# Keys' norm ahead of the scores, one normalisation for eight heads, and a first threshold search counted by ScalarE alone

## The chip, the cores and the metric

One core of a Trainium2 chip runs the whole kernel in one launch. The metric is the device time in microseconds. TensorE (PE) multiplies, VectorE (DVE) and ScalarE (ACT) work on elements, GpSimd (POOL) does the small updates of the threshold search, and SyncE (SP) issues the transfers.

## The reference

The input is 1024 tokens of 1024 features. Two layers of a first block come first, then one second block (a gated recurrence, a chunked linear attention and an MLP), which the change doesn't touch. A layer of the first block, cut to what matters:

```python
def first_block(x, c, ...):
    for l in range(DEPTH):                       # 2
        h = rmsnorm(x, g_pre[l]) * (1.0 + scale) + shift
        p = h @ w_in[l]
        u_val, u_gate, g_conv, c_q, c_kv, k_idx, w_idx, g_attn = jnp.split(p, offsets, axis=-1)
        y_conv = conformer_conv(u_val, u_gate, ...) * jax.nn.silu(g_conv)
        y_attn = dsa_attention(c_q, c_kv, k_idx, w_idx, ...) * jax.nn.silu(g_attn)
        y = jnp.concatenate([y_conv, y_attn], axis=-1) @ w_out[l]
        x = x + gate * rmsnorm(y, g_post[l])

def dsa_attention(...):                          # blocks of 128 queries, 8 heads
    cq = rmsnorm(c_q, q_norm_g)
    kv = rmsnorm(c_kv, kv_norm_g)                # the keys' norm
    score = jnp.einsum("bth,bths->bts", w_b, jax.nn.relu(s_raw))
    _, sel = lax.top_k(score, 256)               # of the keys up to the query
    logits = q . kv[sel] * KV_LORA ** -0.5 + bias
    probs = jax.nn.softmax(logits)
    o = (probs . kv[sel]) @ w_uv                 # 64 outputs a head
```

## The kernel before

SBUF is cut into 50 pages of 1024 words a partition. A page is handed out and freed by the program in the order in which its code is emitted; a page that is freed and handed out again makes its new writer wait for its old readers. fp32 products are three matmuls of a high and a low part (`split`, L262 to L265; `mm3`, L267 to L271). A scheduler puts the emitted instructions of each engine into one fixed order ahead of the run. What it starts from is the order in which generators are woven (`weave`), with rates, gates and priorities in the tables `RATES`, `GATES` and `PRIOR`.

A layer makes the inputs of a convolution, then the latents of queries, keys and index keys (`g_latents`, six units), then index scores for the blocks 2 to 7 of 128 queries (`g_scores`, L844 to L859; the blocks 0 and 1 have at most 256 keys and need no choice). A threshold for each query is searched bit by bit on the two 16-bit halves of the scores, 31 bits in all (`g_topk`). There are two searches a layer, one for the blocks 2, 3 and 4 and one for 5, 6 and 7. In each bit the keys of a block at or above a candidate are counted. The table `GROUPS` says by whom: in the first search block 2 (384 keys) by VectorE (L921, updates in L926, L929 and L931), and blocks 3 and 4 (512 and 640 keys) by ScalarE as a sum of signs (L913), with GpSimd making the next candidate out of the count:

```python
nc.gpsimd.tensor_scalar(hn, half, nxt, None, op0=OP.add)                        # L916
nc.gpsimd.tensor_scalar(tm, cnt, lim, -step, op0=OP.is_gt, op1=OP.mult)         # L917
nc.gpsimd.tensor_tensor(half, tm, hn, op=OP.add)                                # L919
```

In the second search VectorE counts blocks 5 and 6 (768 and 896 keys) and ScalarE block 7. A search ends with the threshold as a float, the choice of ties by a running count, and the mask (L956 to L979). Its pages are freed late, that is, handed out again from the attention on.

After the scores the keys are normed (`norm_keys`: ScalarE's square, a matmul of ones in L302, ScalarE's logarithm L294 and exponential L297, a product), split, and multiplied into the values (L1010). Queries of all heads follow, with both searches running beside. Then comes the attention, a block of 128 queries at a time, in pairs of heads: logits (L1116 to L1124), minimum with the mask (L1130; for the blocks 0 and 1 L1134 and L1137), exponential with its sum (L1138), the reciprocal of the two sums (L1141), its broadcast over 64 rows by two matmuls (L1145), the product with the gate (L1147), transposes (L1154) and their copies (L1158, L1160), the values (L1164), and the final product (L1168). The attention of blocks 0 to 4 has the second search woven in.

## Time and profile before

| | |
|---|---|
| three runs | 3029.22, 3030.16, 3030.83 us |
| median | 3030.16 us |
| span of the profiled execution, its only time on record | 3029.3 us |
| PE, PEld, DVE, ACT, POOL busy | 2906.8, 2362.8, 2229.9, 1679.8, 247.2 us |
| HBM read, written | 201.21, 60.29 MB |

Busy time is that of instructions on an engine; a busy TensorE may still run at its lower clock, which the slices and the windows of the trace give beside it (PEclk, 1.00 is 2.4 GHz and 0.50 is 1.2 GHz). A wait is idle time of an engine just before an instruction, with the instruction that ended it.

### The profile page before, as it was taken

How to read it: one execution, taken by the hardware profiler on the slowest of the kernel's cores; microseconds unless marked ns; L12 is line 12 of the kernel's file. 1: busy time of each engine (PE TensorE's matmuls, PEld its weight loads, DVE VectorE, ACT ScalarE, POOL GpSimd, SP SyncE). 2: the span in 40 equal slices, each digit the busy share in tenths (PEclk: the TensorE clock that was granted, in tenths of full speed). 3: DMA queues.
4: the chain of work that ended last, by engine and by line, in shares of the span. 5: the costliest groups of instructions: out<-in, count | busy, mean ns of one | idle time of the engine just before them, and what ended most of it. 6: DMA issues, size and time to landing. Idle time of an engine off the chain costs nothing.

```text
span 3029.3 us, 40735 instructions
## 1 busy us (share of the span) xinstructions
PE 2906.8 (96%) x15235; PEld 2362.8 (78%) x15235; DVE 2229.9 (74%) x4118; ACT 1679.8 (55%) x3032; POOL 247.2 (8%) x630
## 2 busy tenths in 40 slices
PE   9998787999999888999999999999999999999999
PEld 6877565778877665777888888888888888888887
DVE  5998899776988899756555667656666587776875
ACT  6248766737147866646444466555555654454454
POOL 0005511000005511000000000000000000000000
PEclk9999989999999989999999999999999999999999
DMA  8222102154101200133122211101013344456443
GB/s 276 63 40 63 42 18 77 48 193 149 39 18 42 63 19 18 36 112 118 49 62 62 79 35 36 56 29 56 29 37 122 103 143 153 151 201 238 153 146 111
DMA packets 218637, 264.14 MB, mean 87 GB/s; under 512 B 11504, under 2 KB 153543, under 8 KB 218439
## 3 DMA queue, kind: packets, MB, share of 16 engines
q1 hardware_dynamic: 218438, 261.54, 26.7%
q8 instruction: 119, 1.95, 0.3%
q14 instruction: 80, 0.65, 0.1%
HBM read 201.21 MB, written 60.29 MB: 86 GB/s over the span
## 4 chain that ended last, share of the span: by engine, by line
PE 58%; DVE 5%; POOL 2%; ACT 2%; DMA 1%; issue 1%; POOLq 0%; ACTq 0%
PE ps L269 15%; PE ps L271 15%; PE ps L270 15%; PE ps L331 5%; PE ps L1499 2%; DVE pg L921 2%; POOL consts L917 1%; PE ps L1164 1%; PE ps L1154 1%; POOL consts L919 1%; POOL consts L916 1%; DMA pg<-in_w_in_dram 1%; PE ps L1488 0%; DVE pg L1130 0%; PE ps L498 0%
## 5 line engine op out<-in xcount | busy, mean ns | idle before, releaser
L269 PE MATMUL ps<-pg,pg 128*128 128x512 f32 (+2 forms) x3080 | 1178.7, 384 | 15.1 <-DVE pg L265 4.2
L270 PE MATMUL ps<-pg,pg 128*128 128x512 f32 (+2 forms) x3080 | 1176.3, 383 | 0.0
L271 PE MATMUL ps<-pg,pg 128*128 128x512 f32 (+2 forms) x3080 | 1176.0, 382 | 0.0
L264 ACT ACTIVATE pg<-pg 128x512 fp32r<-128x512 f32 (+2 forms) x884 | 481.7, 591 | 527.7 <-PE ps L271 157.2
L269 PEld LDWEIGHTS ps<-pg,pg 128*128 128x128 f32 x3080 | 580.5, 189 | 132.9 <-DVE pg L265 10.1
L271 PEld LDWEIGHTS ps<-pg,pg 128*128 128x128 f32 x3080 | 580.6, 189 | 109.8 <-issue 3.7
L270 PEld LDWEIGHTS ps<-pg,pg 128*128 128x128 f32 x3080 | 580.8, 189 | 107.9 <-issue 3.5
L265 DVE TENSOR_TENSOR pg<-pg,pg 128x512 fp32r<-128x512 f32 (+2 forms) x884 | 528.2, 636 | 136.4 <-ACT pg L264 121.3
L278 POOL TENSOR_TENSOR consts<-consts 128x1 f32<-128x1 f32 x56 | 31.3, 559 | 2069.0 <-DVE consts L277 2069.0
L913 ACT ACTIVATE pg<-pg,consts 128x512 bf16<-128x512 uint16 (+5 forms) x186 | 166.8, 897 | 40.8 <-POOL consts L919 36.1
L703 DVE SCALAR_TENSOR_TENSOR pg<-pg,consts,pg 128x512 f32<-128x512 f32 (+15 forms) x256 | 176.9, 742 | 0.4
L331 PE MATMUL ps<-pg,pg 128*128 128x512 f32 x768 | 175.9, 389 | 0.0
L921 DVE TENSOR_SCALAR_CACHE_REDUCE pg<-pg,consts 128x384 bf16<-128x384 uint16 (+5 forms) x186 | 170.9, 919 | 2.3
L331 PEld LDWEIGHTS ps<-pg,pg 128*128 128x128 f32 x768 | 143.8, 188 | 29.6
L1138 ACT ACTIVATE pg<-pg,consts 128x256 f32<-128x256 f32 (+7 forms) x128 | 98.9, 774 | 70.2 <-DVE consts L1130 51.7
L1154 PE MATMUL ps<-consts,pg 128*128 128x128 f32 x576 | 107.7, 291 | 1.9 <-ACT pg L1160 1.1
L852 PE MATMUL ps<-pg,pg 128*128 128x512 f32 (+3 forms) x320 | 86.3, 370 | 14.7 <-DVE pg L844 9.4
L1164 PE MATMUL ps<-pg,pg 128*64 128x128 f32 x1152 | 92.5, 292 | 5.8 <-DVE pg L1147 1.7
L1116 PE MATMUL ps<-pg,pg 128*128 128x384 f32 (+5 forms) x192 | 79.4, 415 | 16.2 <-DVE consts L1130 7.9
L1160 ACT ACTIVATE pg<-ps 128x512 f32<-128x512 f32 (+1 forms) x112 | 57.8, 532 | 66.8 <-PE ps L1154 62.4
L917 POOL TENSOR_SCALAR consts<-consts 128x1 f32<-128x1 f32 x186 | 78.0, 419 | 179.1 <-ACT pg L913 173.5
L1164 PEld LDWEIGHTS ps<-pg,pg 128*64 128x64 f32 x1152 | 64.1, 141 | 35.1 <-issue 13.4
(350 smaller groups left out, 3810.7 us busy)
## 6 DMA issues: line engine op xcount, KB each, us to landing
pg<-in_w_in_dram SPq DMA_DIRECT2D x104, 512.0 KB
pg<-hidden SPq DMA_DIRECT2D x56, 512.0 KB
hidden<-pg SPq DMA_DIRECT2D x48, 512.0 KB
pg<-in_w_ada_dram SPq DMA_DIRECT2D x32, 512.0 KB
pg<-in_w_up_dram SPq DMA_DIRECT2D x32, 512.0 KB
pg<-in_w_down_dram SPq DMA_DIRECT2D x32, 512.0 KB
pg<-in_w_out_dram SPq DMA_DIRECT2D x24, 512.0 KB
x<-pg SPq DMA_DIRECT2D x24, 512.0 KB
```

Source lines behind the costliest of these rows:

```text
L264: self.nc.scalar.activation(hi, src, AF.Copy)
L265: self.nc.vector.tensor_sub(lo, src, hi.bitcast(F32))
L269: nc.tensor.matmul(ps, lhsT=wl, rhs=rh, start=first, stop=False)
L270: nc.tensor.matmul(ps, lhsT=wh, rhs=rl, start=False, stop=False)
L271: nc.tensor.matmul(ps, lhsT=wh, rhs=rh, start=False, stop=last)
L331: nc.tensor.matmul(ps, lhsT=w[z][k], rhs=act[y][k][:, a:b], start=k + n == 0, stop=3 * k + n == 3 * kt - 1)
L703: nc.vector.scalar_tensor_tensor(out, x[:, :512 - d], w, prev[:, d:], op0=OP.mult, op1=OP.add)
L913: nc.scalar.activation(junk_a(b), keys[b], AF.Sign, scale=-1.0, bias=col(tk["half"], b), accum_out=col(tk["cnt"], b))
L917: nc.gpsimd.tensor_scalar(col(tk["tm"], b), col(tk["cnt"], b), lim, -step, op0=OP.is_gt, op1=OP.mult)
L921: nc.vector.tensor_scalar(junk_d(b), keys[b], col(tk["cand"], b), None, op0=OP.is_ge, op1=OP.add, accum_out=col(tk["cnt"], b))
L1154: nc.tensor.transpose(pt[:, c:c + 128], Ps[hi][:, j * 128:j * 128 + 128], self.ident)
L1164: nc.tensor.matmul(uv[hi * 64:hi * 64 + 64], lhsT=V[j // 2][:, v:v + 64], rhs=th[:, jj * 256 + hi * 128:jj * 256 + hi * 128 + 128], start= ...
```

## The change

Three parts, and docstrings and comments taken out, which shifts line numbers.

- The keys' norm becomes a seventh unit of `g_latents`, ahead of the scores, with the page and the function table of that generator; `norm_keys` goes.
- The attention gathers the sums of all eight heads of a block in one [128, 8] tile. Reciprocal, broadcast, gate product and final product happen once a block, at the last pair of heads. The values of the four pairs share one PSUM bank.
- `GROUPS` hands block 2 of the first search to ScalarE, in both layers, so that VectorE counts none there. GpSimd's update takes two operations.

```diff
-GROUPS = ((([2], [3, 4]), ([5, 6], [7])), (([2], [3, 4]), ([5, 6], [7])))
+GROUPS = ((([], [2, 3, 4]), ([5, 6], [7])), (([], [2, 3, 4]), ([5, 6], [7])))
...
-            self.sums = [self.const(2) for _ in range(4)]
+            self.sums = [self.const(8) for _ in range(2)]
...
         def g_latents():
...
+            for s in halves:
+                sq = t[:, s]
+                nc.scalar.activation(sq, kv[:, s], AF.Square)
+                ps = self.bank("t", s4)
+                self.sum_rows(ps, [sq])
+                self.bcast_rstd(sq, ps, 128, tab)
+                nc.vector.scalar_tensor_tensor(kv[:, s], kv[:, s], self.vec[f"kv_norm_g{l}"][:, 0:1], sq, op0=OP.mult,
+                                               op1=OP.mult)
+            yield
             self.free(t, cq)
...
-                        nc.gpsimd.tensor_scalar(col(tk["hn"], b), col(tk["half"], b), nxt, None, op0=OP.add)
                         nc.gpsimd.tensor_scalar(col(tk["tm"], b), col(tk["cnt"], b), lim, -step, op0=OP.is_gt,
                                                 op1=OP.mult)
-                        nc.gpsimd.tensor_tensor(col(tk["half"], b), col(tk["tm"], b), col(tk["hn"], b), op=OP.add)
+                        nc.gpsimd.tensor_scalar(col(tk["half"], b), col(tk["half"], b), col(tk["tm"], b), nxt, op0=OP.add,
+                                                op1=OP.add)
...
-        weave((pr(g_latents(), 9), 6), bg=[(conv, RATES[l][1])])
+        weave((pr(g_latents(), 9), 7), bg=[(conv, RATES[l][1])])
...
-        norm_keys()
...
-                    nc.vector.reciprocal(sm, sm)
-                    pu = self.bank("pu", [6])
-                    uv, rb = pu[:, :128], pu[:, 128:256]
-                    for hi in range(2):
-                        nc.tensor.matmul(rb[hi * 64:hi * 64 + 64], lhsT=sm[:, hi:hi + 1].to_broadcast([128, 64]),
-                                         rhs=self.ident, start=True, stop=True)
-                    nc.vector.tensor_mul(gb[:, hp], gb[:, hp], rb)
+                    uv = uvs[:, hp * 128:hp * 128 + 128]
+                    if hp == 3:
+
+                        nc.vector.reciprocal(sm, sm)
+                        rb = self.bank("pt", [4, 5])
+                        for h in range(8):
+                            nc.tensor.matmul(rb[h % 2 * 64:h % 2 * 64 + 64, h // 2 * 128:h // 2 * 128 + 128],
+                                             lhsT=sm[:, h:h + 1].to_broadcast([128, 64]), rhs=self.ident, start=True,
+                                             stop=True)
+                        nc.vector.tensor_mul(gb, gb, rb)
...
                     self.free(Ps)
-                    nc.vector.tensor_mul(yb[:, hp], uv, gb[:, hp])
+                    if hp == 3:
+                        nc.vector.tensor_mul(yb, uvs, gb)
```

What moves is best seen in the order of the instructions. VectorE at the fifth and sixth heads of attention block 0 of layer 0, before; `pg25_220` and `pg28_221` are the pages of their exponentials, `pg18_209` takes the bits of a count, `pg7_212` and `pg6_211` hold keys of the second search, and `consts_58` stands for all small columns:

```order
L1134 TENSOR_TENSOR pg25_220_3075<-ps_62,consts_58 128x128
L1141 RECIPROCAL consts_58<-consts_58 128x2
L921 TENSOR_SCALAR pg18_209_2801,consts_58<-pg7_212_2804,consts_58 128x768
L1137 TENSOR_REDUCE consts_58<-pg25_220_3075 128x1
L921 TENSOR_SCALAR pg18_209_2801,consts_58<-pg6_211_2803,consts_58 128x896
L1147 TENSOR_TENSOR pg8_214_2987<-pg8_214_2987,ps_62 128x128
L1141 RECIPROCAL consts_58<-consts_58 128x2
L929 TENSOR_SCALAR consts_58<-consts_58 128x2
L931 SCALAR_TENSOR_TENSOR consts_58<-consts_58 128x2
L1134 TENSOR_TENSOR pg28_221_3092<-ps_62,consts_58 128x128
L1168 TENSOR_TENSOR pg38_215_2989<-ps_62,pg8_214_2987 128x128
L1137 TENSOR_REDUCE consts_58<-pg28_221_3092 128x1
```
Between the fifth head's logits and the sixth's there are two counts and the small steps of one bit. The same engine with the change, where L985 to L990 are the end of the first search (L974 to L979 before), `pg26_147` and `pg17_148` pages of that search, `pg16_132` a page of scores, and L1131 and L1134 the logits and the minimum:

```order
L978 TENSOR_SCALAR consts_58<-consts_58 128x1
L985 TENSOR_SCALAR pg26_147_1710<-pg16_132_1364,consts_58 128x640
L986 SCALAR_TENSOR_TENSOR pg17_148_1711<-consts_58,pg26_147_1710 128x640
L988 TENSOR_SCALAR pg16_132_1364<-pg16_132_1364,consts_58 128x640
L989 SCALAR_TENSOR_TENSOR pg26_147_1710<-pg17_148_1711,consts_58,pg26_147_1710 128x640
L990 SCALAR_TENSOR_TENSOR pg16_132_1364<-pg26_147_1710,pg16_132_1364 128x640
L1131 TENSOR_TENSOR pg17_221_3027<-ps_62,consts_58 128x128
L1131 TENSOR_TENSOR pg26_220_3006<-ps_62,consts_58 128x128
L1134 TENSOR_REDUCE consts_58<-pg17_221_3027 128x1
```
The sixth head's page is `pg26_220`, the place of the first search's `pg26_147`, and the seventh's is `pg17_221`, the place of `pg17_148`; both are written behind the last step of the first search.

ScalarE among the latents of layer 1, before; L294 and L297 are the logarithm and the exponential of a norm, L689 the gates, L264 splits, L843 copies of index queries:

```order
L294 ACT_TABLE_LOAD
L294 ACTIVATE pg14_485_6772<-ps_62,consts_58 128x512
L297 ACT_TABLE_LOAD
L297 ACTIVATE pg14_485_6772<-pg14_485_6772 128x512
L264 ACTIVATE pg4_481_6768<-pg32_473_6618 128x512
L264 ACTIVATE pg13_482_6769<-pg25_474_6619 128x512
L726 ACTIVATE pg14_495_7144<-pg27_487_6809 128x15
L689 ACT_TABLE_LOAD
L689 ACTIVATE pg6_493_6850<-ps_62 128x512
L843 ACTIVATE pg18_492_6837<-ps_62 128x384
```
And with the change, where L808 is the square of the keys' norm:

```order
L294 ACT_TABLE_LOAD
L294 ACTIVATE pg14_484_6604<-ps_62,consts_58 128x512
L808 ACTIVATE pg14_484_6604<-pg15_460_6303 128x512
L297 ACT_TABLE_LOAD
L297 ACTIVATE pg14_484_6604<-pg14_484_6604 128x512
L294 ACT_TABLE_LOAD
L294 ACTIVATE pg14_484_6604<-ps_62,consts_58 128x512
L297 ACT_TABLE_LOAD
L297 ACTIVATE pg14_484_6604<-pg14_484_6604 128x512
L264 ACTIVATE pg4_480_6600<-pg23_472_6450 128x512
L264 ACTIVATE pg24_481_6601<-pg25_473_6451 128x512
L808 ACTIVATE pg14_484_6604<-pg15_460_6303 128x512
```
A gate of the conv branch (L689) lies in the middle of norms in both, and with the change a load of a function table stands ahead of every logarithm and every exponential here.

## Rows read from the trace of the kernel before

**Rows 1.** The page: the span, the busy time by engine with its share of the span and the number of instructions, and, out of the slices, PE's busy tenths and its granted clock.

```profile
span 3029.3 us, 40735 instructions
...
PE 2906.8 (96%) x15235; PEld 2362.8 (78%) x15235; DVE 2229.9 (74%) x4118; ACT 1679.8 (55%) x3032; POOL 247.2 (8%) x630
...
PE   9998787999999888999999999999999999999999
...
PEclk9999989999999989999999999999999999999999
```
**Rows 2.** The timeline of ScalarE, start and duration in us: the last score's eviction, the first and the sixth exponential of attention block 0, in layer 0.

```profile
313.50 1.01 ACT L854 ACTIVATE pg<-ps 128x1024 f32<-128x1024 f32 x1
...
397.09 0.40 ACT L1138 ACTIVATE pg<-pg,consts 128x128 f32<-128x128 f32 x1 [1.31 <-DVE consts L1137]
...
406.91 0.40 ACT L1138 ACTIVATE pg<-pg,consts 128x128 f32<-128x128 f32 x1 [0.65 <-DVE consts L1137]
```
**Rows 3.** Busy time of each engine in the four stages of layer 0 that these starts cut, and of layer 1 cut at the same instructions: the length, then PE, weight loads, DVE, ACT, POOL with their instructions, PE's granted clock, the DMA share and GB/s.

```profile
232.50:314.50 82.00, 73.02 (x319) 58.76 (x318) 69.62 (x162) 66.50 (x132) 51.80 (x113) 0.98 0.20 58
...
314.50:397.10 82.60, 60.28 (x220) 42.10 (x219) 70.70 (x169) 66.30 (x131) 38.80 (x109) 0.89 0.14 42
...
397.10:406.90 9.80, 7.68 (x37) 6.15 (x35) 9.37 (x33) 4.14 (x14) 0.64 (x3) 0.50 0.01 2
...
406.90:506.80 99.90, 86.89 (x637) 64.63 (x637) 95.05 (x302) 66.65 (x151) 14.76 (x59) 0.90 0.18 53
...
925.00:1007.40 82.40, 74.74 (x336) 60.80 (x335) 76.94 (x181) 69.98 (x142) 59.62 (x128) 1.00 0.20 61
...
1007.40:1080.50 73.10, 59.99 (x223) 42.75 (x221) 61.92 (x146) 60.27 (x119) 31.53 (x92) 0.90 0.15 48
...
1080.50:1094.70 14.20, 11.53 (x57) 8.87 (x56) 13.59 (x45) 7.19 (x21) 1.92 (x9) 0.50 0.00 0
...
1094.70:1200.00 105.30, 89.69 (x636) 62.88 (x635) 98.31 (x316) 72.36 (x161) 14.58 (x56) 0.96 0.06 18
```
**Rows 4.** Waits in total, number and longest: from 200 to 560 us (layer 0) three of PE and one of ScalarE, then from 880 to 1220 us (layer 1) two of PE.

```profile
PE ps L302 <- ACT pg L294: 12.6, 1, 12.6
...
PE ps L1145 <- DVE consts L1141: 7.5, 8, 1.6
...
PE ps L852 <- DVE pg L844: 3.8, 5, 1.2
...
ACT pg L913 <- POOL consts L919: 17.7, 24, 1.5
...
PE ps L302 <- ACT pg L294: 8.3, 1, 8.3
...
PE ps L1145 <- DVE consts L1141: 8.9, 10, 2.2
```
**Rows 5.** The timeline of PE around the matmul of ones, layer 0.

```profile
346.24 2.07 PE L302 MATMUL ps<-pg,consts 128*128 128x512 f32 x2 [12.62 <-ACT pg L294]
...
349.39 0.63 PE L270 MATMUL ps<-pg,pg 128*128 128x512 f32 x1
...
349.82 0.63 PE L271 MATMUL ps<-pg,pg 128*128 128x512 f32 x1
...
354.87 0.39 PE L270 MATMUL ps<-pg,pg 128*128 128x512 f32 x1
```
**Rows 6.** The timeline of ScalarE: two counts, of 512 and of 640 keys, and a table load with what starts behind it.

```profile
252.59 0.71 ACT L913 ACTIVATE pg<-pg,consts 128x512 bf16<-128x512 int16 x1
...
254.00 0.82 ACT L913 ACTIVATE pg<-pg,consts 128x640 bf16<-128x640 int16 x1
...
193.34 1.28 ACT L689 ACT_TABLE_LOAD   x1
...
194.63 0.60 ACT L689 ACTIVATE pg<-ps 128x512 f32<-128x512 f32 x1
```
**Rows 7.** Groups of VectorE's instructions from 200 to 560 us, shapes apart: total busy, mean ns of one, idle time before.

```profile
L921 DVE TENSOR_SCALAR_CACHE_REDUCE pg<-pg,consts 128x384 bf16<-128x384 uint16 x16 | 9.7, 606 | 0.2
...
L921 DVE TENSOR_SCALAR_CACHE_REDUCE pg<-pg,consts 128x768 bf16<-128x768 int16 x15 | 15.1, 1008 | 0.3
...
L921 DVE TENSOR_SCALAR_CACHE_REDUCE pg<-pg,consts 128x896 bf16<-128x896 int16 x15 | 17.1, 1141 | 0.2
...
L1147 DVE TENSOR_TENSOR pg<-pg,ps 128x128 f32<-128x128 f32 x25 | 7.1, 284 | 2.1 <-PE ps L1145 1.7
...
L1168 DVE TENSOR_TENSOR pg<-ps,pg 128x128 f32<-128x128 f32 x24 | 6.9, 286 | 1.2 <-PE ps L1164 1.1
...
L1158 DVE COPY pg<-ps 128x512 f32<-128x512 f32 x10 | 6.8, 686 | 2.2 <-PE ps L1154 1.8 <-PE ps L1164 0.5
...
L1141 DVE RECIPROCAL consts<-consts 128x2 f32<-128x2 f32 x25 | 4.0, 159 | 0.0
```
**Rows 8.** The timeline of VectorE in layer 1: the first and the last step of the end of the first search.

```profile
1039.23 0.17 DVE L934 TENSOR_SCALAR consts<-consts 128x2 f32<-128x2 f32 x1 [2.02 <-POOL consts L919]
...
1051.84 0.82 DVE L979 SCALAR_TENSOR_TENSOR pg<-pg,pg 128x640 f32<-128x640 bf16 x1
```
**Rows 9.** Groups of GpSimd's instructions from 200 to 560 us.

```profile
L916 POOL TENSOR_SCALAR consts<-consts 128x1 f32<-128x1 f32 x93 | 34.9, 376 | 65.3 <-DVE consts L952 36.2 <-DVE consts L902 21.5
...
L919 POOL TENSOR_TENSOR consts<-consts 128x1 f32<-128x1 f32 x93 | 32.2, 347 | 7.8
```

More of the change, by code (lines that the diff above doesn't have):

```diff
@@ L981, in g_topk @@
             self.free(cnt_pg, kps, late=True)
-        def norm_keys():
-            kv = lat["kv"]
-            t = self.page()
-            tab = self.ln_table()
-            for s in halves:
-                sq = t[:, s]
-                nc.scalar.activation(sq, kv[:, s], AF.Square)
-                ps = self.bank("k", [3])
-                self.sum_rows(ps, [sq])
-                self.bcast_rstd(sq, ps, 128, tab)
-                nc.vector.scalar_tensor_tensor(kv[:, s], kv[:, s], self.vec[f"kv_norm_g{l}"][:, 0:1], sq, op0=OP.mult,
-                                               op1=OP.mult)
-            self.free(t)
         def split_keys():
```

16 lines of the change are left out of this document (9 added, 7 removed).

## The prediction

> **What bounds the kernel now.** I read the page first: busy time by engine, then the slices. PE is busy 2906.8 of 3029.3 us [rows 1], so the whole reads as a kernel bound by TensorE, and an edit that takes work from VectorE or ScalarE seems worth nothing. The slices say more: PE falls to 7 or 8 tenths in slices 4 to 7 and 14 to 16, and its granted clock to 8 tenths in slices 6 and 15 [rows 1]. The change touches only the sparse attention of the two layers, so I cut those two pieces into four stages by what starts on ScalarE [rows 2], the end of the last score's eviction, the first, and the sixth exponential of attention block 0, and took the busy time of each engine in each stage [rows 3]. What the reader is to see there, layer 0: the scores (82.00 us, PE 73.02); from the last score to the first exponential (82.60 us, with PE 60.28, VectorE 70.70 and ScalarE 66.30, so no engine full, and the clock at 0.89); the first five heads (9.80 us, VectorE 9.37, clock 0.50, which is the lower level, 1.2 GHz); then attention proper (99.90 us, VectorE 95.05, PE 86.89). Layer 1 is alike: 82.40, 73.10, 14.20, 105.30. Last I read which wait PE names in them [rows 4]: one wait of the ones-matmul of the keys' norm for ScalarE's logarithm, 12.6 and 8.3 us, and the reciprocal's broadcast for VectorE, 7.5 and 8.9 us. Behind the long wait PE runs at the lower clock: matmuls of a 512-wide product start 0.43 us apart and take 0.63 each, and only from 354.87 on 0.39 [rows 5], so of the 8.6 us from 346.24 some 3 are lost as well.
>
> **Part by part.** All sums stand against the profiled span of 3029.3 us; the median of the runs is 3030.16, so I add 0.9 at the end.
>
> Keys' norm. Its place between the scores and the values goes, and with it the wait: in layer 0 12.6 + 3 = 15.6 us of a stage that otherwise held 67 us; in layer 1 8.3 + about 2 by the stage's clock of 0.90. What is late next in this stage is ScalarE. I walked ScalarE's order of the changed kernel with the durations of the trace: a Sign count takes 0.71 us at 512 keys, 0.82 at 640 [rows 6], thus an estimated 0.61 at 384. From the last score to the first exponential this sums to 60.5 us in layer 0 (64.2 before), 59.3 in layer 1 (59.1 before): fewer bits of the old blocks, but one count more in each bit. VectorE falls from 66.6 to 39.5 us there. With ScalarE filled to 95% (VectorE reaches 95.05 of 99.90 where it sets the pace [rows 3]) the stage takes about 64 us in layer 0 and 63 in layer 1. That is -18 and -10; bounds -20 and -8 in layer 0 (the latter if the counts wait for GpSimd as now, 17.7 us in all [rows 4]), -13 and -2 in layer 1.
>
> In its new place the norm has Square, two ones-matmuls, logarithm, exponential, scale. The work is the same, but ScalarE's order shows other loads of function tables: one less in layer 0, three more in layer 1, where gates of the conv branch fall between logarithm and exponential. A load takes 1.28 us and the next activation starts 1.29 us after it [rows 6]. So -1.3 and +3.8 us of ScalarE time; since the index latents wait for ScalarE just there, and a wait of PE brings the lower clock behind it, I take +2 and +5; bounds 0 and +8 each.
> The Trainium skill (ScalarE: Activation LUTs, What ACT_TABLE_LOAD costs) gives 1283 ns for the load and about 1380 ns of drain on top, 2.66 us in all. The row agrees with the load and shows no drain behind it; by the rule the two net loads would be worth an estimated 5.3 us, by the row 2.6.
>
> One normalisation for eight heads. Per block of 128 queries four gate products of 0.284 us, four final products of 0.286 and four reciprocals of 0.159 [rows 7], 2.9 us of VectorE, become one each. A 512-wide product out of PSUM isn't in the trace; nearest is the 512-wide copy out of PSUM, 0.686, and four times the narrow one, 1.14, is the other bound. So 0.16 + 2 x 0.686 = 1.5 us, a gain of 1.4 us a block (0.5 at the other bound), 11 us for eight blocks. Matmul count stays at eight 128x128 broadcasts. On PE's path the waits for the reciprocal (7.5, 8.9) go for three pairs in four.
>
> Counts to ScalarE. 31 counts of 384 keys with their updates leave VectorE: the 0.61 of a count less the overlap of 0.08, the update's share, some 27 us a layer with the normalisation by VectorE's order summed with traced durations (2023 to 1969 us over both layers). 31 x 0.61 = 19 us a layer come to ScalarE. ScalarE has the room in total, but not in the last 60 us ahead of attention. So the first search ends later: before, its last count lies some 36 us of ScalarE work ahead of the first exponential; now it lies 14 and 7 us behind it. This meets memory. The page of the sixth head of attention block 0 is the one that holds the counts and the ties of the first search (page 26), and VectorE's new order has the whole end of that search, L985 to L990 for three blocks, ahead of the sixth head's logits. So five heads start as early as they can and the sixth waits. VectorE's work from first to sixth head is 9.3 us before and 30.4 (layer 1: 31.4) now: six or seven bits of the second search, a 768 and an 896 count of 1.01 and 1.14 us with updates each [rows 7], and the end of the first search, from 1039.23 to 1052.66 in layer 1 with 2 us of other work in it [rows 8]. At 95% and with a handover to ScalarE and back: 34 us and 35 us where there were 9.80 and 14.20, +24 and +21. Bounds +20 and +17 (VectorE full) to +28 and +26. PE has nothing else to do there.
> What VectorE does in that gap it need not do later: by the order, seven to eight bits of the second search are done early, 2.25 us each, 17 us, and 11 us come from the normalisation. But behind the sixth head PE is soon the bound: 86.89 busy of 99.90 at clock 0.90, so 78 us at full clock and 22 to be had; in layer 1 89.69 at 0.96 of 105.30, 86 and 19. Of it I take two thirds, -15 and -13, since the start still runs at the low clock after the gap; the least is the reciprocal's wait, -8 each, the most -22 and -19.
>
> GpSimd. Three operations become two, but with three blocks six remain for each bit. Their first (hn, mean 0.376 us [rows 9]) was already done beside the count, off the path; the last, 0.347, becomes a form with a pointer. I take 0; a path shorter or longer by 0.1 us over 31 bits gives 3 us a layer at most either way. Scores: VectorE freer, PE waits for its share of copies 3.8 us now [rows 4]; ScalarE gets the counts in exchange: 0, bounds -3 and +3.
>
> Sum, layer 0: -18 + 2 + 24 - 15 = -7. Layer 1: -10 + 5 + 21 - 13 = +3. Together -4, with 0.9: 3026 us. The gain and its price nearly cancel.
>
> **Rivals.**
> It pays in full (faster). If the end of the first search comes sooner than I walked, because its counts no longer wait for GpSimd, the gap is at its floor (+20, +17) and attention behind it gets all that PE leaves (-22, -19): -20 + 0 + 20 - 22 = -22 and -13 + 4 + 17 - 19 = -11, 2997 at its end; halfway from the even case about 3012. For it: VectorE is 95% busy in attention, and 54 us are taken from it. Against: the bits it does early it does while PE starves.
> The Trainium skill (Perfetto Trace Analysis, Optimizing Scalar/DVE Operations) says that where VectorE is saturated, moving work to ScalarE may make sense. The stage of the first search isn't that case (70.70 of 82.60), the attention stage is.
> The gap decides (slower). Place: the sixth head's page, in both layers. Price +24 to +28 and +21 to +26, and attention gains only the reciprocal's waits (-8 each), because PE, restarted at the low clock, and not VectorE is the bound there; the first stage gains -15 and -6. Layer 0 -15 + 3 + 26 - 8 = +6, layer 1 -6 + 6 + 24 - 8 = +16: about 3052. It decides as soon as attention gives back less than the gap costs beyond the first stage's gain, that is under 24 us over both layers (24 + 21 + 2 + 5 - 18 - 10).
> The wait moves and doesn't go (within noise to slower): the norm in the latents stalls PE there by the 8 to 12 us that it stalled it later, since Square, logarithm and exponential queue on ScalarE behind the splits of the queries' latents. Then +8 each in place of +2 and +5: 3035. Against: nothing of the scores needs the keys.
>
> **How the numbers follow.** About even 0.40 (own range 3014 to 3040), paid in full 0.30, gap decides 0.22, wait moved 0.08. What a measurement can tell from no change is 0.2%, 6 us, so 3024 to 3036. Of the even case 0.20 is within, 0.12 faster, 0.08 slower; of the last 0.06 within. Paid in full is faster, but for 0.02. This gives faster 0.40, same 0.28, slower 0.32 with rounding. The range runs from the full gain, 2999, to the gap case with a little over, 3054.
>
> **What would show it.** Right: no wait of the ones-matmul over 4 us between scores and values, the stage from last score to first exponential near 64 us in both layers, then a stretch of 30 us or more after the fifth exponential with PE all but empty and VectorE at L985 to L990, and attention behind it shorter by 15 us. Wrong: exponentials of the sixth head within 20 us of the first (the full gain); or an attention stage as long as now (the gap decides); or a new PE wait of 8 us among the latents.

## The result and the profile after

The changed kernel takes 3047.46 us (median of four, 3044.54 to 3052.91) where the kernel before takes 3030.02 beside it: a ratio of 1.0060, with a 95% interval of 1.0045 to 1.0074. It is slower; 3026 was forecast. The profiled execution spans 3051.1 us, 21.8 more than that of before; it is the longest of the four, while the medians differ by 17.4. The page, span, busy times, PE's busy tenths and its granted clock, to be read against [rows 1]:

```profile
span 3051.1 us, 40435 instructions
...
PE 2890.5 (95%) x15235; PEld 2365.5 (78%) x15235; DVE 2181.9 (72%) x3724; ACT 1708.6 (56%) x3158; POOL 230.2 (8%) x568
...
PE   9996967999999968999999999999999999999999
...
PEclk9998979999999979999999999999999999999999
```
TensorE's matmuls, VectorE and GpSimd are less busy in total, and the kernel is slower: PE's low slices have become fewer and deeper, 6, 6 and 7 in slices 4, 6 and 7. The stages tell where. The table cuts both traces at the same instructions of ScalarE: the start of the first score's eviction (ScalarE's copy of a score out of PSUM), the end of the last one, the first, sixth and last exponential of a layer's attention (us, from the timelines).

| stage | before, layer 0 | after | | before, layer 1 | after | |
|---|---|---|---|---|---|---|
| scores | 117.2 | 131.3 | +14.1 | 114.9 | 108.3 | -6.6 |
| last score to first exponential | 82.6 | 66.7 | -15.9 | 73.1 | 64.8 | -8.3 |
| first to sixth exponential | 9.8 | 36.5 | +26.7 | 10.1 | 36.6 | +26.5 |
| sixth to last exponential | 210.7 | 193.9 | -16.8 | 201.4 | 188.4 | -13.0 |
| to the next layer's first score, or the end | 274.9 | 284.4 | +9.5 | 1737.3 | 1742.8 | +5.5 |

Busy time of each engine in layer 0, columns as in [rows 3]: the scores before, then after the first four stages of the table, with the stretch 246.00 to 268.80 out of the scores as the second of their lines:

```profile
197.30:314.50 117.20, 108.22 (x491) 87.99 (x490) 102.40 (x213) 85.38 (x168) 52.80 (x115) 0.99 0.27 63
...
197.50:328.80 131.30, 105.12 (x482) 88.03 (x483) 104.78 (x150) 82.42 (x173) 35.85 (x87) 0.90 0.25 57
246.00:268.80 22.80, 1.10 (x6) 0.58 (x4) 22.66 (x36) 0.10 (x2) 0.00 (x0) 0.62 0.06 18
328.80:395.60 66.80, 60.57 (x235) 43.23 (x234) 42.13 (x93) 59.58 (x139) 29.39 (x88) 0.97 0.16 51
395.60:432.00 36.40, 13.26 (x53) 10.19 (x53) 34.02 (x90) 25.99 (x62) 14.48 (x42) 0.55 0.00 0
432.00:625.90 193.90, 171.67 (x1345) 130.73 (x1345) 160.75 (x354) 133.38 (x259) 12.10 (x38) 0.97 0.19 60
```
The stage ahead of attention gained what it should, and behind the sixth exponential attention gained too. Two places lost most. The first is the gap between the fifth and sixth head; the second lies in the scores of layer 0, where nothing had been expected. The stretches behind attention lost 9.5 and 5.5. The waits of PE there and in the gaps, layer 0 (180 to 560 us) and then layer 1, which answer to [rows 4]:

```profile
PE ps L862 <- ACT pg L864: 26.5, 2, 25.4
...
PE ps L1113 <- DVE pg L1131: 22.9, 5, 20.8
...
PE ps L1143 <- DVE consts L1140: 1.0, 1, 1.0
...
PE ps L1113 <- DVE pg L1131: 23.1, 4, 21.0
```
The ones-matmul's wait of 12.6 and 8.3 us is gone, and of the reciprocal's 7.5 us in layer 0 there is 1.0 left. In their place stand 25.4 us in one piece for a score's eviction, and 20.8 and 21.0 for a head's page. First the scores, ScalarE and then VectorE, layer 0:

```profile
245.27 0.72 ACT L904 ACTIVATE pg<-pg,consts 128x512 bf16<-128x512 int16 x1
...
268.79 1.02 ACT L864 ACTIVATE pg<-ps 128x1024 f32<-128x1024 f32 x1 [22.70 <-DVE consts L906]
...
247.24 19.87 DVE L703 SCALAR_TENSOR_TENSOR pg<-pg,consts,pg 128x512 f32<-128x512 f32 x30
...
267.68 1.02 DVE L869 SCALAR_TENSOR_TENSOR pg<-pg,consts,pg 128x768 f32<-128x768 f32 x1
...
268.62 0.21 DVE L906 TENSOR_SCALAR consts<-consts 128x1 f32<-128x1 f32 x2
```
ScalarE has counted block 3 for the sign and sits idle for 22.70 us with an eviction of scores next in its queue, until 268.79. The trace names VectorE's L906, the search's first step, started at 268.62; but the eviction doesn't read what L906 writes. By the program it waits for a page: it writes the one (`pg15_145`) that VectorE's L869, a sum of scores, has yet to read, and L869 ends at 268.70. Both stand on VectorE behind a run of taps of the convolution (L703, an instruction for each tap, 30 of them in the trace here, 19.87 us), and the order of both engines is fixed. In the 22.8 us of the window 246.00 to 268.80 above, VectorE is busy 22.66, ScalarE 0.10 and PE 1.10. By VectorE's order 186 taps stand ahead of the first search's first step, and so ahead of these sums; before there were 141 ahead of that step.

And the gap of layer 0, ScalarE, PE and VectorE in turn:

```profile
395.56 0.40 ACT L1135 ACTIVATE pg<-pg,consts 128x128 f32<-128x128 f32 x1 [3.33 <-DVE consts L1134]
...
406.46 0.39 ACT L1135 ACTIVATE pg<-pg,consts 128x128 f32<-128x128 f32 x1
...
432.04 0.39 ACT L1135 ACTIVATE pg<-pg,consts 128x128 f32<-128x128 f32 x1
...
408.68 0.33 PE L1153 MATMUL ps<-consts,pg 128*128 128x128 f32 x1
...
429.82 0.69 PE L1113 MATMUL ps<-pg,pg 128*128 128x256 f32 x2 [20.82 <-DVE pg L1131]
...
417.43 0.16 DVE L945 TENSOR_SCALAR consts<-consts 128x3 f32<-128x3 f32 x1
...
428.74 0.82 DVE L990 SCALAR_TENSOR_TENSOR pg<-pg,pg 128x640 f32<-128x640 bf16 x1
...
429.48 0.48 DVE L1131 TENSOR_TENSOR pg<-ps,consts 128x128 f32<-128x128 f32 x2
```
PE stands from 409 to 429.82; VectorE, busy 34.02 of the 36.40 us, does bits of the second search until 417.43, then the end of the first until 429.5, and then at once the logits that were waiting.

### The profile page after: what moved, and what is told of

Same layout as the page of the kernel before. It is cut to its first block, busy times and chain, and to the rows that moved or that the text cites. A ratio compares the mean times of both kernels' runs of the same rounds, so it can differ in the third digit from the quotient of the medians.

```text
span 3051.1 us, 40435 instructions
## 1 busy us (share of the span) xinstructions
PE 2890.5 (95%) x15235; PEld 2365.5 (78%) x15235; DVE 2181.9 (72%) x3724; ACT 1708.6 (56%) x3158; POOL 230.2 (8%) x568
## 4 chain that ended last, share of the span: by engine, by line
PE 74%; DVE 14%; ACT 5%; DMA 2%; issue 2%; POOL 2%; SPq 0%; POOLq 0%; ACTq 0%; DVEq 0%
PE ps L269 19%; PE ps L270 18%; PE ps L271 18%; PE ps L331 5%; DVE pg L932 4%; DVE pg L703 3%; PE ps L1499 2%; PE ps L1163 2%; PE ps L1153 2%; ACT pg L924 2%; PE ps L862 1%; DVE pg L265 1%; DVE pg L1127 1%; POOL consts L929 1%; PE ps L1113 1%
## 5 line engine op out<-in xcount | busy, mean ns | idle before, releaser
L269 PE MATMUL ps<-pg,pg 128*128 128x512 f32 (+2 forms) x3080 | 1176.8, 384 | 13.2 <-ACT pg L264 3.8
L270 PE MATMUL ps<-pg,pg 128*128 128x512 f32 (+2 forms) x3080 | 1176.3, 383 | 1.3 <-DVE pg L265 1.3
L271 PE MATMUL ps<-pg,pg 128*128 128x512 f32 (+1 forms) x3080 | 1175.2, 383 | 0.0
L264 ACT ACTIVATE pg<-pg 128x512 fp32r<-128x512 f32 (+2 forms) x884 | 481.4, 591 | 532.7 <-PE ps L271 159.7
L269 PEld LDWEIGHTS ps<-pg,pg 128*128 128x128 f32 x3080 | 580.7, 189 | 133.7 <-DVE pg L265 11.8
L270 PEld LDWEIGHTS ps<-pg,pg 128*128 128x128 f32 x3080 | 581.1, 189 | 110.2 <-DVE pg L265 3.6
L271 PEld LDWEIGHTS ps<-pg,pg 128*128 128x128 f32 x3080 | 580.8, 189 | 107.9 <-issue 2.9
L924 ACT ACTIVATE pg<-pg,consts 128x384 bf16<-128x384 uint16 (+7 forms) x248 | 204.6, 825 | 18.6 <-POOL consts L929 16.3
L703 DVE SCALAR_TENSOR_TENSOR pg<-pg,consts,pg 128x512 f32<-128x512 f32 (+15 forms) x256 | 173.2, 737 | 1.3 <-PE ps L271 0.8
L331 PEld LDWEIGHTS ps<-pg,pg 128*128 128x128 f32 x768 | 143.9, 188 | 29.7
L932 DVE TENSOR_SCALAR_CACHE_REDUCE pg<-pg,consts 128x768 bf16<-128x768 uint16 (+1 forms) x124 | 133.5, 1077 | 3.0
L1135 ACT ACTIVATE pg<-pg,consts 128x384 f32<-128x384 f32 (+7 forms) x128 | 98.6, 771 | 58.4 <-DVE consts L1127 50.1
L927 POOL TENSOR_SCALAR consts<-consts 128x1 f32<-128x1 f32 x248 | 90.3, 364 | 331.2 <-ACT pg L924 310.4
L1153 PE MATMUL ps<-consts,pg 128*128 128x128 f32 x576 | 101.4, 290 | 8.2 <-ACT pg L1135 5.1
L1113 PEld LDWEIGHTS ps<-pg,pg 128*128 128x128 f32 x192 | 39.7, 208 | 87.8 <-DVE pg L1131 49.0
L929 POOL TENSOR_SCALAR consts<-consts 128x1 f32<-128x1 f32 x248 | 102.5, 413 | 23.1
L869 DVE SCALAR_TENSOR_TENSOR pg<-pg,consts,pg 128x512 f32<-128x512 f32 (+5 forms) x84 | 78.7, 949 | 32.4 <-ACT pg L864 31.3
```

The costliest lines, as they stand in the source:

```text
L264: self.nc.scalar.activation(hi, src, AF.Copy)
L269: nc.tensor.matmul(ps, lhsT=wl, rhs=rh, start=first, stop=False)
L270: nc.tensor.matmul(ps, lhsT=wh, rhs=rl, start=False, stop=False)
L271: nc.tensor.matmul(ps, lhsT=wh, rhs=rh, start=False, stop=last)
L331: nc.tensor.matmul(ps, lhsT=w[z][k], rhs=act[y][k][:, a:b], start=k + n == 0, stop=3 * k + n == 3 * kt - 1)
L703: nc.vector.scalar_tensor_tensor(out, x[:, :512 - d], w, prev[:, d:], op0=OP.mult, op1=OP.add)
```

## The experiments

Times are medians; each is compared with the kernel before on the same chip. Experiments that are compared with one another may come from different chips, on which the kernel before took 3028.19 to 3032.39 us. "Stage" is the one from the last score to the first exponential, "attention" the one from the sixth to the last exponential, and the bits of the second search that lie ahead of some instruction are told by VectorE's counts of 768 keys.

**The parts alone.** The norm, with the latents' seventh unit:

```diff
+            for s in halves:
...
+            yield
             self.free(t, cq)
...
-        weave((pr(g_latents(), 9), 6), ...
+        weave((pr(g_latents(), 9), 7), ...
...
-        norm_keys()
```

> The keys' norm moved into the latents and nothing else. Theory (two costs, in different parts): the seventh unit of the latents pulls the convolution forward, so that VectorE's order has 186 instead of 141 taps ahead of the first search's first step in layer 0, and ScalarE, and behind it PE, wait there; the gap at the sixth head comes from the groups and is absent here. Then the scores of layer 0 are some 14 us longer, the stalls of 12.6 and 8.3 us go: 3020 to 3030 in all, with a PE wait of about 20 us for the score evictions. Rival (all of the loss is the gap at the sixth head's page): no such wait, 3005 to 3015.

Measured: 3048.15, ratio 1.0060 (1.0045 to 1.0075), above both ranges. The wait is here, 23.6 us in one piece, and the scores of layer 0 are 22.9 us longer. The stage gains 17.1 and 11.0, and attention loses 10.5 and 7.4: most of the gain was handed back.

The normalisation alone (`g_attn` and `sums` as in the change):

> The one normalisation for eight heads and nothing else (the column hn shares its place with neg, for room). Theory: 7.5 and 8.9 us of waits for the reciprocal go in most part and VectorE loses 1.4 us a block: 3015 to 3025. Rival (attention is set by PE, the waits are taken up elsewhere): 3026 to 3032.

Measured: 3024.21, 0.9981 (0.9972 to 0.9991), faster. Attention is 9.9 and 4.4 us shorter, and 4.6 and 4.5 come back in the stretch behind it; why isn't shown.

The groups with GpSimd's two steps (`GROUPS`, and the two operations as in the change):

> Block 2 of the first search counted by ScalarE, and GpSimd in two steps, nothing else. Theory: the gap at the sixth head (26 us in each layer in the changed kernel) is here in full, with no earlier first exponential to pay for it, since the norm's stall stays: 3040 to 3060. Rival (the loss is the taps ahead of the search, made by the norm's new place): 3015 to 3032.

Measured: 3069.53, 1.0137 (1.0120 to 1.0154): the worst, and worse than expected. The first exponential comes 22.6 and 6.8 us sooner after the first score, but the gap has 30.0 and 22.5 us, and attention behind it is longer by 17.5 and 19.0, since VectorE did none of the second search's bits ahead of the first exponential (five before).

Norm and normalisation, with the old groups:

> The norm in the latents and the one normalisation, with the old groups and the old three steps of GpSimd. Theory: the sum of the two parts alone, with the wait behind the taps in layer 0 and no gap: 3012 to 3026. Rival (the gap isn't made by the groups): 3040 or more.

Measured: 3045.18, 1.0050 (1.0035 to 1.0065). The time is the rival's, but there is no gap: so the gap is the groups', and groups and two steps together account for some 2 of the 17 us only (what each of them does alone follows below). The loss is near the sum of the norm's and the normalisation's, +18.3 and -5.6.

**Mendings of the changed kernel.** Pages:

```diff
-        self.settle()
         PT, GP = self.pages(2)
...
             for b in blocks:
+                if b == 2:
+                    self.settle()
```

> The changed kernel, but the three pages of the first search are handed out again only from attention block 2 on, so that the sixth head of block 0 takes a page that earlier heads have left. Theory: the gap of 36 us between the first and the sixth exponential falls to some 12 us in both layers; part of it comes back later, since the bits of the second search that VectorE did in the gap are still to do: 3015 to 3035. Rival (ScalarE's counts set the pace there, the page is only where it shows): attention slows by what the gap loses, 3043 to 3050.

Measured: 3044.22, 1.0048 (1.0033 to 1.0063). The stretch from first to sixth exponential falls from 36.5 to 11.8 us and from 36.6 to 12.1, and attention behind it lengthens by 20.8 and 21.7 against the changed kernel. The page was the wait; what was waited for, the first search's end and its bits, still had to be done. The rival was right on the time.

Taps:

```diff
-            yield
             self.free(t, cq)
...
-        weave((pr(g_latents(), 9), 7), ...
+        weave((pr(g_latents(), 9), 6), ...
```

> The changed kernel with the norm in the latents but without a unit of its own (no yield behind it, six units as before), so that the convolution isn't pulled forward: 141 taps ahead of the first search, as before. Theory: the PE wait of 25.4 us for a score's eviction in layer 0 goes, and 12 to 16 us with it: 3030 to 3036. Rival (the wait comes from ScalarE's own counts): the wait stays, 3044 to 3050.

Measured: 3041.74, 1.0041 (1.0026 to 1.0055). The scores of layer 0 are shorter by 19.4 us, and the gap behind the fifth head is 51.0 us in place of 36.5: VectorE does there the bits that it did in the stage before. The wait has gone as the theory said, but three quarters of its gain went into the gap, and the time lies between the two ranges.

Both:

> Both edits in the changed kernel: pages of the first search back from block 2 on, and no unit for the norm. Theory: both costs go, 3000 to 3022, faster than before. Rival (something third holds the time, such as ScalarE's load or the table loads): 3030 or more.

Measured: 3031.95, 1.0007 (0.9998 to 1.0017): the kernel before, not faster. Without both costs the change is worth nothing, so the rest of the forecast's gain was wrong too. VectorE in the stage and behind the sixth exponential:

```profile
308.90:375.70 66.80, 59.99 (x240) 44.04 (x239) 34.96 (x65) 59.37 (x142) 36.95 (x94) 0.95 0.15 48
386.10:459.00 72.90, 56.73 (x397) 42.83 (x397) 69.80 (x204) 54.90 (x131) 15.65 (x46) 0.89 0.06 19
```
VectorE is busy 34.96 of 66.80 us where ScalarE has 59.37, and then 69.80 of 72.90. The first search ends 36 us behind the first exponential; in the kernel before it ended 30 us ahead of it.

Norm without a unit, normalisation, old groups and three steps:

> The kernel before with the norm in the latents without a unit of its own and with the one normalisation; old groups, three steps of GpSimd. Theory: faster than the same with a seventh unit by the 10 to 15 us of the taps: 3000 to 3013. Rival (the taps cost nothing where VectorE counts block 2): the same time as with a seventh unit.

Measured: 3029.56, 0.9999 (0.9990 to 1.0008). It is 15.6 us faster than with the unit, as much as was expected of the taps, though above 3000 to 3013, and 5 us slower than the normalisation alone, 4.6 of them between the attention of layer 0 and the first score of layer 1, where the norm of layer 1 now lies: the norm's new place doesn't pay even without the taps.

**Was the stall on the path?** The kernel before without the keys' norm, which leaves out a part of the computation and is there for its time alone:

```diff
-        norm_keys()
```

> The kernel before with the keys' norm left out altogether, square, ones-matmuls, logarithm, exponential and product. Theory (the stall of PE was VectorE's time for bits of the second search, which it now does during attention at some 2.2 us a bit): the stage from last score to first exponential shortens by 10 to 17 us, as it did with the norm in the latents, and attention lengthens by 5 to 11 us in each layer; 3015 to 3027 in all. Rival (the stall was on the path): 3000 to 3010, attention as long as before.

Measured: 3029.57 beside 3029.62, ratio 0.9997 (0.9988 to 1.0007). With all of the norm gone, and the wait of 12.6 and 8.3 us with it, nothing is gained, and the time lies above the theory's range too: the stage is 12.8 and 4.0 us shorter, attention 11.2 and 7.0 longer. PE's next wait in the stage is that of the values for ScalarE's copy, in one piece:

```profile
PE ps L1010 <- ACT pg L1011: 9.1, 1, 9.1
```
So the stall that the trace showed as the longest of PE was worth nothing. In layer 0 VectorE had used it: nine bits of the second search lie ahead of the sixth exponential before, three here, and six bits at some 2 us are the 11.2 us. In layer 1 there is one bit less only, and 7.0 us come back all the same.

**Are early bits worth anything?** One number in `PRIOR`, the same in both layers, on three kernels:

```diff
-PRIOR = ((-30, 0, 0, -200, 100, ...
+PRIOR = ((-30, 0, 0, 0, 100, ...
```

> The norm in the latents without a unit of its own, the one normalisation, the old groups, and the second search's priority in the scheduler's order raised from -200 to 0, so that by VectorE's order 11 of its bits in place of 3 lie ahead of the sixth head in layer 0, and 9 in place of 7 in layer 1. Theory (VectorE is the bound from the first exponential on, 2.2 us a bit, while it has room ahead of it): attention some 17 and 5 us shorter, the stage ahead of it 4 to 8 us longer, 3012 to 3024 where the same without the priority is 3029.6. Rival (attention is bound by PE or ScalarE): 3027 to 3036.

> The changed kernel with both mendings (no unit for the norm, the first search's pages back from attention block 2 on) and the second search's priority raised from -200 to 0: 15 bits in place of 3 ahead of the sixth head in layer 0, 15 in place of 10 in layer 1. Theory: VectorE is idle half of the stage ahead of attention (35 of 67 us busy) and full in it, so the bits cost little there and free 2.2 us each later; ScalarE has 1.14 us for block 7 in each, so the stage is longer by 5 to 12 us: 3010 to 3026 where the same without the priority is 3032. Rival (ScalarE is the bound throughout, so that order gives nothing): 3030 to 3040.

> The one normalisation alone, with the second search's priority raised from -200 to 0; the norm's stall stays. 10 bits in place of 8 ahead of the sixth head in both layers. Theory: 4 us less attention in a layer, 3015 to 3023 where the same without the priority is 3024.2. Rival (the priority by itself makes the gain, whatever the bits): as much gain here as in the kernels with more bits moved, under 3012.

Measured: 3034.17 (1.0014, 1.0005 to 1.0024), 3043.77 (1.0040, 1.0025 to 1.0055) and 3032.41 (1.0007, 0.9997 to 1.0016): each slower than its kernel with the old priority, by 4.6, 12 and 8 us. In the first, layer 0, eleven bits in place of four lie ahead of the sixth exponential; the stage is 15.5 us longer and attention 15.7 shorter. A bit costs 2.2 us on either side. My theory had seen room ahead of attention because VectorE was idle there, and fell.

**What is left open, tested one by one.** An empty seventh unit in the kernel before:

```diff
+                yield
             self.free(t, cq)
...
-        weave((pr(g_latents(), 9), 6), ...
+        weave((pr(g_latents(), 9), 7), ...
```

> The kernel before with an empty seventh unit among the latents (the keys' norm stays where it was): VectorE's order has 186 instead of 141 taps of the convolution ahead of the first search of layer 0, and nothing else is meant to change. Theory (the unit and not the norm makes the long wait in the scores): scores of layer 0 longer by 12 to 23 us with a PE wait of some 20 us for a score's eviction, 3036 to 3048. Rival (the norm's own work on ScalarE makes it): 3026 to 3033.

Measured: 3059.87 beside 3032.39, 1.0086 (1.0071 to 1.0101). One empty unit costs 27 us, more than expected: 19.8 in the scores of layer 0 and 9.9 in the stage of layer 1 (the latter isn't explained). PE's waits from 190 to 340 us, the first 23.6 us in one piece:

```profile
PE ps L853 <- ACT pg L855: 24.0, 2, 23.6
```
The unit alone makes the wait: with each unit of the latents the convolution is carried on by its rate of two steps, so a seventh unit, empty or not, puts two more steps of taps ahead of the searches.

The groups with late pages:

> Block 2 of the first search counted by ScalarE and GpSimd in two steps, alone (3069.5), with the first search's pages handed out again only from attention block 2 on. Theory (the gap behind the fifth head is the page's wait, and in this kernel VectorE stands idle in it): the gaps of 30 and 22 us shrink to about 10, 3045 to 3056. Rival (the page only shows the wait): 3064 or more. In both, 15 us or more over the kernel before stay, since VectorE does none of the second search's bits ahead of the first exponential.

Measured: 3054.83 beside 3032.39, 1.0071 (1.0056 to 1.0086). The gaps shrink to 7.8 and 7.3 us, and late pages take back about half of that kernel's loss; attention stays longer by 30.8 and 27.1 us. The trace says what makes it longer. From the sixth exponential of layer 0 to the end of the second search:

```profile
384.10:515.60 131.50, 95.13 (x634) 68.51 (x635) 126.45 (x387) 86.17 (x187) 21.03 (x62) 0.84 0.13 39
```
VectorE is busy 126.45 of 131.50 us, where the kernel before had 95.05 of 99.90 [rows 3]: 31.4 us more of its work, and 30.8 us more of attention. None of the second search's bits lies ahead of the sixth exponential, nine did before, and the first search ends 26 us behind the first exponential.

GpSimd's two steps with the old groups:

> GpSimd's update in two steps, with the old groups, and nothing else. Theory: the step that goes was off the path, 3027 to 3032. Rival (the new form with a pointer is slower by 0.1 us or more on the path of a bit): 3033 to 3040; (shorter): 3020 to 3026.

Measured: 3019.65 beside 3032.39, 0.9946 (0.9930 to 0.9963): faster by more than any other part, where I had put 0. GpSimd in the kernel before, and then with two steps, in the same stretch:

```profile
338.30 0.19 POOL L919 TENSOR_TENSOR consts<-consts 128x1 f32<-128x1 f32 x1
338.57 0.22 POOL L916 TENSOR_SCALAR consts<-consts 128x1 f32<-128x1 f32 x1
338.89 0.30 POOL L917 TENSOR_SCALAR consts<-consts 128x1 f32<-128x1 f32 x1
339.28 0.19 POOL L919 TENSOR_TENSOR consts<-consts 128x1 f32<-128x1 f32 x1
339.56 0.22 POOL L916 TENSOR_SCALAR consts<-consts 128x1 f32<-128x1 f32 x1
```
```profile
339.51 0.30 POOL L916 TENSOR_SCALAR consts<-consts 128x1 f32<-128x1 f32 x1 [1.44 <-ACT pg L913]
339.90 0.30 POOL L918 TENSOR_SCALAR consts<-consts 128x1 f32<-128x1 f32 x1
340.90 0.30 POOL L916 TENSOR_SCALAR consts<-consts 128x1 f32<-128x1 f32 x1 [0.69 <-ACT pg L913]
341.29 0.30 POOL L918 TENSOR_SCALAR consts<-consts 128x1 f32<-128x1 f32 x1
```
Before, operation follows operation with some 0.09 us between, the step of one block (L916, 0.22) ahead of another block's answer (L917): the queue was full, and a step that nobody waited for held up one that ScalarE did wait for. With two steps GpSimd waits for ScalarE. From 200 to 560 us, GpSimd's two groups and ScalarE's wait for them:

```profile
L918 POOL TENSOR_SCALAR consts<-consts 128x1 f32<-128x1 f32 x93 | 45.6, 491 | 8.7
L916 POOL TENSOR_SCALAR consts<-consts 128x1 f32<-128x1 f32 x93 | 45.1, 485 | 164.8 <-ACT pg L913 163.4
...
ACT pg L913 <- POOL consts L918: 13.1, 24, 1.4
```
ScalarE's wait falls from 17.7 [rows 4] to 13.1 us, though the two operations that a block has to wait for take longer on average (0.485 and 0.491 us; before L917 had 0.408 and L919 0.347): the gain is the third operation's place in the queue, not a shorter path. PE's wait for the norm falls from 12.6 to 3.8 us by this alone, and scores and stage together are shorter by 9.0 and 5.8.

Block 6 of the second search to ScalarE, on the normalisation alone, in `GROUPS` for both layers:

```diff
-([5, 6], [7])
+([5], [6, 7])
```

> The one normalisation (3024.2), with block 6 of the second search moved from VectorE to ScalarE; the first search stays as it was. Theory (a bit of the second search costs 2.2 us of VectorE wherever it stands, and attention has VectorE at 93% and ScalarE at 65%): VectorE's bit falls to 1.1 us, attention 8 to 20 us shorter in each layer, 2995 to 3015. Rival (ScalarE becomes the bound as in the first search, or PE is): 3024 to 3040.

Measured: 3054.46 beside 3032.39, 1.0069 (1.0054 to 1.0084), some 27 us slower than without it by the ratios, and outside both ranges. The same stretch of layer 0, sixth to last exponential, in the normalisation alone and with the block moved; each is followed by its two parts, cut where ScalarE's last count of the second search ends, and by the exponentials of the first part:

```profile
408.90:609.60 200.70, 179.10 (x1357) 135.96 (x1357) 175.12 (x395) 134.95 (x260) 16.45 (x59) 0.93 0.19 56
...
408.90:507.10 98.20, 82.92 (x636) 64.17 (x636) 93.78 (x260) 66.58 (x152) 15.97 (x57) 0.92 0.19 58
507.10:609.60 102.50, 96.18 (x723) 71.79 (x721) 81.33 (x135) 68.37 (x110) 0.49 (x2) 0.95 0.19 55
...
L1139 ACT ACTIVATE pg<-pg,consts 128x256 f32<-128x256 f32 (+4 forms) x35 | 22.5, 644 | 17.6 <-DVE consts L1131 11.1 <-DVE consts L1138 6.4
...
405.10:620.20 215.10, 186.22 (x1358) 139.80 (x1358) 149.03 (x316) 165.93 (x323) 44.34 (x151) 0.90 0.18 53
...
405.10:522.00 116.90, 93.26 (x639) 69.82 (x639) 72.06 (x188) 98.34 (x215) 43.49 (x149) 0.81 0.18 57
522.00:620.20 98.20, 92.97 (x720) 69.98 (x719) 76.97 (x129) 67.59 (x110) 0.85 (x3) 1.00 0.17 48
...
L1139 ACT ACTIVATE pg<-pg,consts 128x256 f32<-128x256 f32 (+4 forms) x35 | 22.4, 640 | 2.1 <-DVE consts L1138 1.9
```
VectorE has 26.1 us less to do and ScalarE 31.0 more, and over the whole stretch neither looks full. Cut in two, it does. As long as the second search runs, VectorE is busy 93.78 of 98.20 us without the move; behind it PE is, 96.18 of 102.50. With the block moved VectorE has 72.06 of 116.90 us of the first part and ScalarE 98.34; the exponentials, which had waited 17.6 us for VectorE, wait 2.1, and stand behind counts in ScalarE's own queue; the part is 18.7 us longer. So the move doesn't show that VectorE was not the bound of attention: it was nearly full in the first part, and the move put ScalarE in its place at a higher price, as the rival had it. That ScalarE's queue sets the pace there is read from these rows and not tested.

**The best version.** Normalisation and two steps, and the same with the norm in the latents without a unit:

> The one normalisation and GpSimd's update in two steps, old groups, keys' norm where it was. Theory (the two gains lie in different stages, GpSimd's queue in the scores, the normalisation in attention, and add): 3010 to 3017, faster than either alone. Rival (what one gains ahead the other gives back, as with the norm): 3018 to 3026.

> The same with the keys' norm in the latents, without a unit of its own. Theory (the norm's stall was time that the searches used, and is worth nothing): 3012 to 3024, no faster than with the norm in its old place. Rival (with GpSimd freer the searches no longer need the stall, and the norm's new place pays): 3000 to 3009.

Measured, five runs each beside 3028.19: 3012.62 (0.9946, 0.9932 to 0.9959) and 3015.95 (0.9957, 0.9945 to 0.9970). The first is the fastest kernel here. That the two gains add isn't shown: two steps alone have the same ratio. The norm's new place again gives nothing. Its kernel with the groups of the change and late pages is the one with both mendings, at 1.0007: moving block 2 to ScalarE costs some 15 us even there; attention is longer by 9.0 and 12.9 us, where the end of the first search now falls, and the stretches ahead of it give some of that back.

## Why the prediction was wrong

The forecast was about even, 3026, with faster at 0.40 and slower at 0.32; the time lies inside the range, clear of no change, and on the slow side. That it lies inside is owed to the range, which ran from the full gain to the gap, and not to the account: none of the rivals had the taps. Cut as the forecast's sum is, the profile has +8.3 for -7 in layer 0, +8.1 for +3 in layer 1, and +5.5 behind that, which had no term. By its own steps:

- **Scores: "0, bounds -3 and +3"** is the step that failed by most. Measured +14.1 in layer 0. I had weighed what VectorE and ScalarE have to do there, and not what stands ahead of what: the `yield` behind the norm, for which the diff's `6` became `7`, moved 45 taps of the convolution ahead of the first search and of the sums of scores beside it, and I had VectorE's order at hand and read it only at the sixth head. The empty unit shows the cause (27 us in the kernel before), and the two pairs with and without it its price in the change, 12 us with late pages, 6 without. In layer 1 the scores are 6.6 us shorter, of which GpSimd's two steps alone give 5.0.
- **GpSimd: "I take 0", because the step that goes was "already done beside the count, off the path"** failed too. It was off the path of its own block and on that of the others, in one queue (ScalarE's wait for GpSimd falls from 17.7 to 13.1 us without it); 52 of 82 us busy [rows 3] didn't look full, but the gaps between 113 operations belong to it as well. Alone it gives 13 us by the medians.
- **Keys' norm: -18 and -10 in the stage.** Measured -15.9 and -8.3: right in the stage, and wrong as a term of the sum, since the stall was no loss. Leaving the norm out gives 0.0 by the medians. I had taken VectorE's fall from 66.6 to 39.5 us in the stage for room, where it was work pushed behind.
- **The gap: +24 and +21**, worked out as 34 and 35 us long. Measured 36.5 and 36.6: the mechanism, the place and the length were right. In layer 1 I had set it against 14.20 us, which reached to the seventh exponential; the sixth comes after 10.1, so the price is +26.5. It also rests on the first search's last count, put 14 and 7 us behind the first exponential; it ends 20 and 12 us behind it.
- **Attention behind it: -15 and -13.** Measured -16.8 and -13.0. This agrees, and the rows bear out the reason given: 15 bits lie ahead of the sixth exponential where nine did before (15 and eight in layer 1), the normalisation takes its part, and PE limits what is left. In the kernel before VectorE was busy 95.05 of 99.90 us up to the end of the second search [rows 3], and behind it PE 102.84 of 110.80:

```profile
506.80:617.60 110.80, 102.84 (x745) 74.60 (x744) 87.21 (x168) 70.40 (x112) 0.00 (x0) 0.97 0.17 51
```
  The two thirds of PE's room were a guess, and that they fit to 2 us is luck.
- **The latents: +2 and +5.** In layer 0 the first score starts 0.2 us later; to the first score of layer 1 there are +9.5, of which 4.6 go with the normalisation alone (4.6 there) and 4.6 with the norm (9.2 with both, 6.6 with the norm and its unit alone): right for the norm, while what comes back behind attention, 4.6 and in the tail about as much, had no term in the sum.
- **One normalisation: 1.4 us a block.** A 512-wide product out of PSUM takes 0.684 us, the reciprocal 0.198:

```profile
L1146 DVE TENSOR_TENSOR pg<-pg,ps 128x512 f32<-128x512 f32 x8 | 5.5, 684 | 2.9 <-PE ps L1143 2.9
...
L1140 DVE RECIPROCAL consts<-consts 128x8 f32<-128x8 f32 x8 | 1.6, 198 | 0.0
```
  The nearest row had 0.686, so the durations were right. But VectorE's busy time, which counts what overlaps once, falls with the normalisation alone by 9.8 us for both layers (2229.9 to 2220.1), where the sum of durations had 22: instructions behind one another overlap (in the lines on the scores L906 starts 0.08 us before L869 ends), and I had taken that off for the counts only. The kernel gains 5.6 us in all.
- **Of the rivals**, the one named "the gap decides" came nearest in time, 3052, and not in cause: it had the gap's price right, but attention gave back 16.8 and 13.0 for its 8 each, and the scores and the stretches behind attention cost about as much as that. The rule of the Trainium skill (Perfetto Trace Analysis, Optimizing Scalar/DVE Operations) that offloading to ScalarE may make sense where VectorE is saturated was put beside attention's 95%; with block 6 moved there, the trace doesn't bear it out (VectorE's busy time falls from 93.78 to 72.06 us while the second search runs, and that part is 18.7 us longer).
- **The table loads**: the load of 1.28 us with the next activation right behind it, in layer 1 after, at 896.94 and 898.23, agrees with the row ahead of the prediction; of the drain that the Trainium skill adds (ScalarE: Activation LUTs, What ACT_TABLE_LOAD costs) nothing shows behind it, nor ahead of it, where the activation before ends at 896.92.

Along one chain of kernels from before to after the loss splits into normalisation -6, norm in the latents +5, groups, two steps and late pages +2, the seventh unit +12, early pages +4, which make +17 by construction. The price of a part depends on what else is in the kernel: the seventh unit costs 27, 16, 12 or 6 us in the four pairs that were run.

What stays open: the groups cost some 38 us by the ratios without the other two parts and some 15 with them. In layer 0 the rows tell the two apart (without them no bit lies ahead of the sixth exponential where nine did, with them there are four in either kernel of the pair), but why the scheduler's order puts none there isn't shown. Nor was it tested by itself whether a count in ScalarE's queue holds up the exponentials behind it, as the rows with block 6 moved suggest.

## What to carry to other kernels

A long wait of one engine can be worth nothing, as long as the others use the time for work that must be done anyway; leave the waited-for work out once, and the time says what the wait is worth (fixed orders change with it, so look where the other engines' work went). A busy share over a long stretch hides a full engine: cut the stretch where the limit changes, here at the end of the second search. Where orders are fixed ahead, every unit that drives an interleaving is part of the change: read the order of each engine over the whole stretch, not only where the change is meant to act. And a small engine's queue is full when its operations follow each other, whatever its busy share says; a step that nobody waits for still delays those behind it.

## What was not expected of the hardware

The same GpSimd operation on one column takes from 0.205 to 1.214 us in layer 0 of the kernel before (L916, median 0.222, mean 0.376 [rows 9]), and with two steps both forms take 0.30 in the lines above, where GpSimd waits for ScalarE between them, but 0.485 and 0.491 on average. What lengthens the others wasn't tried.
